# Experts' weights in a ring of 35 buffers in strict order of use, the norm's factor applied per place, two pairs put back at once

## The chip, the cores and the metric

The kernel runs on one core of one Trainium2 chip. The metric is device time in microseconds (us), the median of three runs. Engine names are those of the profile: PE (TensorE), PEld (its weight load), DVE (VectorE), ACT (ScalarE), POOL (GpSimd), SP (SyncE, whose queue issues every load and store of this kernel).

## The reference, cut to what matters

Two transformer-like blocks run one after the other on 256 tokens of width 1024, all in float32. The second ends in a mixture of experts: each token goes to the best of four groups and there to two of eight experts, so 32 experts of 1024 x 512 in all.

```
x = x + merged @ w_out
x = x + hier_moe(rms_norm_2(x, g_ffn), ...)

def hier_moe(h, w_group, b_group, w_expert, b_expert, w_gate, w_up, w_down):
    g_prob = softmax(hf @ w_group + b_group);  g_idx = argmax(g_prob)
    e_prob = softmax(the group's 8 of (hf @ w_expert + b_expert))
    top_p, top_i = top_k(e_prob, 2)
    combine = sum(one_hot(8 * g_idx + top_i, 32) * top_w)
    for e in range(32):
        hid = silu(t @ w_gate[e]) * (t @ w_up[e])
        out = out + combine[:, e:e + 1] * (hid @ w_down[e])
```

## The kernel before

The two blocks fill the first 1290 us or so of the program; there weights are loaded into five buffers `wraw`, split into a high and a low part (`whi` on ACT, `wlo` on DVE or POOL) and multiplied. The last step of the second block is the product with `w_out`, whose eight loads are the last ones ahead of the experts.

The mixture of experts is the function `moe`. Each expert has 64 places (`CAP`), and two experts make a pair `p` of 128 places, so there are 16 pairs.

- **The router** (under `HPR`) turns `x` into `Thi`/`Tlo` (`tsplit`), sums its squares (L1354), and multiplies it by the router's weights. The norm's factor `rs` is made on POOL (L291). Then a chain of some fifty DVE instructions on 2 to 64 numbers per partition finds groups, experts, weights (`comb`) and each token's rank in its expert. Its last result besides the ranks is `oi` (L1548), a flag that says whether an expert has more than 64 tokens; SP reads it into a register (`nc.values_load`, L1549), and a branch at the program's end runs the rare rest.
- **The rows to gather** are `hh` and `hl`, the high and low part of `x * g_ffn * rs`. DVE makes `x * g_ffn` into `hs` in transposed order (L1355); then `rs` is applied (`hh` on ACT, L1377; `hl` on DVE, L1378).
- **`prepare(q)`** makes one-hot matrices for two pairs, gathers their tokens by matmul into `xg`, and reads each place's weight `cg`.
- **`hidden(p)`** multiplies `xg` by the gate and up weights of two experts, 16 loads of 512 KB, and ends in a silu and a product with `cg`. **`down(p)`** transposes the result and multiplies it by the down weights, 8 loads of 512 KB. **`scatter`** puts the 128 places back into `x`.
- **`fetch`** issues such a load. Its buffer comes from `ring()`, which goes round a string of letters: 5 `wraw`, 5 `whi`, 4 `wlo`, 5 `wx`, 5 `u`, 4 `Thi`, 4 `Tlo`, in all 32 buffers, most of which the program's earlier parts use too. So 32 x 12 = 384 loads are issued by SP, in the order that the scheduler chooses by priority (`HPM`) and by when it thinks that a buffer is free.

All of SP's work is one queue: an instruction that waits holds those behind it.

Of the kernel before, what the change touches and what calls it, by code (L numbers as in the profile page):

```python
# [28 lines left out]
OP = mybir.AluOpType  # L29
# [4 lines left out]
RAW, WHI, WLO = 5, 5, 4  # L34
RAWX = 5

# [4 lines left out]
CAP = 64  # L41
RING = "w" * 5 + "h" * 5 + "l" * 4 + "x" * 5 + "u" * 5 + "T" * 4 + "t" * 4

# [76 lines left out]
def tile_model(ctx: ExitStack, tc: tile.TileContext, I: dict, out: bass.AP):  # L120
# [1202 lines left out]
    def moe(router, wb, ring):  # L1323
# [14 lines left out]

        hs, hh, hl = [unit(True), unit(True)], [runit(True), runit(True)], [runit(True), runit(True)]
        hk, hlk = ([h.rearrange("q (k p) -> q k p", k=8) for h in hx] for hx in (hh, hl))  # L1340
        hp = [h.rearrange("q (k p) -> q p k", k=8) for h in hs]
        wrs, rb = router
# [4 lines left out]
        with tc.high_priority(HPR):  # L1347

            for c in range(2):
                for t in range(2):  # L1350
                    cs = slice(512 * c, 512 * c + 512)
                    tsplit(x[:, t, cs], t, pair[c])
                    sq = wtile([128, 512], F32, name="th")
                    S.activation(sq, x[:, t, cs], AF.Square, accum_out=ss[:, t, c:c + 1])  # L1354
                    V.tensor_mul(hp[t][:, 64 * c:64 * c + 64, :], x[:, t, cs].rearrange("q (p k) -> q p k", k=8),  # L1355
                                 wb[:, cs].rearrange("q (p k) -> q p k", k=8))
            ps = psum.tile([128, 512], F32, name="proj", bufs=3)
            for K in range(8):
# [45 lines left out]
            m32 = wtile([128, 2, 32], F32R, name="m32", bufs=1)  # L1404
            comb = R_(32, "comb")

            def spread(dst, src):
                for t in range(2):
                    V.tensor_tensor(dst[:, t].rearrange("p (g e) -> p g e", g=4),
                                    ohg[:, t, :, None].to_broadcast([128, 4, 8]),  # L1410
                                    src[:, t, None, :].to_broadcast([128, 4, 8]), op=OP.mult)

            spread(m32, member)
            pc = psum.tile([128, 512], F32, name="proj", bufs=3)
# [18 lines left out]
        def prepare(q):  # L1433

            oh = wtile([128, 2, 4, CAP], F32R, name="oh", bufs=1)
            for t in range(2):
                full = [128, 4, CAP]
                V.tensor_tensor(oh[:, t], cnt_row[:, None, :].to_broadcast(full),
                                rank[:, t, 4 * q:4 * q + 4, None].to_broadcast(full), op=OP.is_equal)
            ohv = oh.rearrange("p t a s -> p t (a s)")  # L1440
            xg = []
            for k0 in range(0, 8, 2):
                if k0 % 4 == 0:
                    xg.append(unit().rearrange("p (k s) -> p k s", k=4))
                tp = psum.tile([128, 4, 128], F32, name="tp", bufs=2).rearrange("p (k a) s -> p k (a s)", k=2)
                for k in range(2):
                    for n, (src, t) in enumerate(((hk, 0), (hlk, 0), (hk, 1), (hlk, 1))):
                        mm(tp[:, k, :], src[t][:, k0 + k, :], ohv[:, t], n == 0, n == 3)
                (S.copy if k0 % 4 else V.tensor_copy)(xg[-1][:, k0 % 4:k0 % 4 + 2, :], tp)
            got = []  # L1450
            for a in range(2):
                rows = [ohv[:, t, 128 * a:128 * a + 128].bitcast(F32) for t in range(2)]
                tp = psum.tile([128, 4, 128], F32, name="tp", bufs=2)
                for t in range(2):
                    T.transpose(tp[:, t, :], rows[t], ident)
                for t in range(2):
                    mm(tp[:, 2, 0:2], rows[t], comb[:, t, 4 * q + 2 * a:4 * q + 2 * a + 2], t == 0, t == 1)
                ohT = wtile([128, 2, 128], F32R, name="ohT", bufs=4)
                S.copy(ohT, tp[:, 0:2])
                cg = wtile([128, 1], F32, name="cg", bufs=4)  # L1460
# [3 lines left out]
            return got  # L1464

        def fetch(nme, e, i):
            with tc.high_priority(HPM):
                w = ring()
                src = I[nme][0, e]
                if nme == "w_down_2":  # L1470
                    nc.sync.dma_start(w, src.rearrange("(p k) n -> p k n", k=4)[:, i])
                else:
                    nc.sync.dma_start(w.rearrange("p (j n) -> p j n", j=2),
                                      src.rearrange("(p a j) n -> p a j n", a=4, j=2)[:, i])
            return w
# [3 lines left out]
        def hidden(p, xg, a, cg):  # L1479
# [9 lines left out]
            hid = wtile([128, 512], F32, name="th")  # L1489
            S.activation(hid, pg, AF.Silu)  # L1490
            V.scalar_tensor_tensor(hid, hid, cg, pu, op0=OP.mult, op1=OP.mult)  # L1491
            return hid

        def down(p, hid):
            tp = psum.tile([128, 4, 128], F32, name="tp", bufs=2)
            hv = hid.rearrange("s (p k) -> s k p", k=4)
            for k in range(4):
                T.transpose(tp[:, k, :], hv[:, k, :], ident)
            hT = wtile([128, 4, 128], F32, name="hT", bufs=2)
            S.copy(hT, tp)  # L1500
# [11 lines left out]

        def scatter(yh, yl, ohT):
# [14 lines left out]

        ready, back = prepare(0), None
        for p in range(16):  # L1530
            xg, a, cg, ohT = ready.pop(0)
            hid = hidden(p, xg, a, cg)
            if back is not None:
                scatter(*back)
            if not ready and p < 15:
                ready = prepare(p // 2 + 1)
            back = *down(p, hid), ohT
        scatter(*back)
        store()

# [9 lines left out]
        with tc.If(flag > 0):  # L1550
            V.tensor_scalar(rank, rank, float(CAP), None, op0=OP.is_gt)
            V.tensor_mul(comb, comb, rank)
            turn, mine = wtile([128, 1], F32, name="turn", bufs=1), R_(32, "mine")
# [9 lines left out]
            with tc.For_i(0, 32) as e:  # L1563
                V.tensor_scalar(turn, turn, 1.0, None, op0=OP.add)
                V.tensor_scalar(tm, cnt_row[:, 0:32], turn[:, 0:1], None, op0=OP.is_equal)
                V.tensor_tensor(mine, comb, tm[:, None, :].to_broadcast([128, 2, 32]), op=OP.mult)
                V.tensor_reduce(cw, mine, axis=AX.X, op=OP.add)
                at = lambda nme: I[nme][0, bass.ds(e, 1)].rearrange("o a b -> (o a) b")
                for t in range(2):
# [10 lines left out]
                    hid = wtile([128, 512], F32, name="th")  # L1580
                    S.activation(hid, pg, AF.Silu)
                    V.scalar_tensor_tensor(hid, hid, cw[:, t:t + 1], pu, op0=OP.mult, op1=OP.mult)
                    hT = wtile([128, 4, 128], F32, name="hT", bufs=2)
                    tp = psum.tile([128, 4, 128], F32, name="tp", bufs=2)
# [15 lines left out]
    def run_moe(router, wb):  # L1600
# [8 lines left out]
                     t=lambda: flat(act.tile([128, 4, 256], F32, name="Tlo", bufs=4)),  # L1609
                     x=lambda: extra.tile([128, 1024], F32, name="wx", bufs=RAWX), u=unit)  # L1610
        turns = [0]
# [44 lines left out]
```

## Time and profile before

| What | Value |
|---|---|
| Time, median of 3 runs | 1817.86 us (1817.31 to 1818.43) |
| The profiled execution: own time, span | 1818.63 us, 1816.9 us |
| PE busy | 1696.3 us (93%) |
| DVE, ACT, POOL busy | 1029.8, 714.2, 324.9 us |
| Read from HBM over the span | 387.50 MB, 214 GB/s in the mean |
| SP's loads, share of 16 DMA engines | 62.8% |

The span runs from the first instruction to the last; the own time is what the run of that execution reported, 1.73 us more. PE's busy time is partly modelled: a PE that waits for weights in small steps is shown as busy.

### The profile page before, as it was taken

The numbers are of one execution on the slowest core, as the hardware profiler recorded it, in microseconds if no ns is written. First come the engines' busy times: TensorE is split into PE (matmuls) and PEld (weight loads), VectorE is DVE, ScalarE is ACT, GpSimd is POOL, SyncE is SP. The second block draws the span as 40 slices with busy tenths as digits, with TensorE's granted clock in tenths as the row PEclk, the third lists the DMA queues.
The fourth block names the chain that finished last, engine by engine and source line by source line (L and its number), as shares of the span: only waits on it lengthen the run. The fifth ranks groups of instructions, "written<-read, shape, count | busy, mean of one in ns | idle before, by whom it ended". The sixth has DMA issues, their size and how long they took to land.

```text
span 1816.9 us, 24162 instructions
## 1 busy us (share of the span) xinstructions
PE 1696.3 (93%) x9005; PEld 1262.6 (69%) x9005; DVE 1029.8 (57%) x1664; ACT 714.2 (39%) x1359; POOL 324.9 (18%) x247
## 2 busy tenths in 40 slices
PE   7999999999999999999998988867799999999997
PEld 6999888888798899888877767745644343343332
DVE  7656657656664577765768899798712121121121
ACT  5556555645444655655546452413311110110010
POOL 1111117120102002311034443464200000000000
PEclk9999999999999999999999999988899999999999
DMA  8645454465466443453745533124799999999993
GB/s 251 194 133 149 135 152 123 139 197 166 142 185 202 134 138 118 122 174 111 233 165 170 154 93 94 47 93 144 277 382 379 409 409 407 409 408 409 407 380 154
DMA packets 186105, 390.17 MB, mean 215 GB/s; under 512 B 28609, under 2 KB 66689, under 8 KB 185985
## 3 DMA queue, kind: packets, MB, share of 16 engines
q1 hardware_dynamic: 185984, 388.60, 62.8%
q8 instruction: 72, 1.18, 0.3%
q14 instruction: 49, 0.39, 0.1%
HBM read 387.50 MB, written 1.05 MB: 214 GB/s over the span
## 4 chain that ended last, share of the span: by engine, by line
PE 74%; DVE 10%; DMA 10%; issue 2%; POOL 2%; ACT 1%; SPq 0%; DVEq 0%; ACTq 0%; POOLq 0%
PE proj L146 54%; PE sc L146 10%; PE pv L146 5%; DMA u<-in_w_gate_dram 3%; DMA wraw<-in_w_gate_dram 2%; PE tp L146 2%; DVE wlo L214 2%; PE tp L362 1%; PE tp L283 1%; DMA whi<-in_w_gate_dram 1%; DVE u L934 1%; DMA wraw<-in_w_in_dram 1%; DMA wlo<-in_w_up_dram 1%; DMA wlo<-in_w_down_dram 1%; DMA Tlo<-in_w_gate_dram 1%
## 5 line engine op out<-in xcount | busy, mean ns | idle before, releaser
L213 ACT CAST whi<-wraw 128x1024 fp32r<-128x1024 f32 x336 | 352.0, 1052 | 317.6 <-PE proj L146 274.8
L214 DVE TENSOR_TENSOR wlo<-wraw,whi 128x1024 fp32r<-128x1024 f32 (+1 forms) x285 | 372.0, 1308 | 169.1 <-PE proj L146 117.2
L146 PE MATMUL proj<-wlo,Thi 128*128 128x512 f32 (+1 forms) x1056 | 418.4, 397 | 5.8 <-DVE wlo L214 5.7
L146 PE MATMUL proj<-whi,Thi 128*128 128x512 f32 (+1 forms) x1056 | 417.8, 398 | 3.6 <-ACT P L985 1.0
L146 PE MATMUL proj<-whi,Tlo 128*128 128x512 f32 (+1 forms) x1056 | 415.2, 396 | 1.5 <-DVE Tlo L968 1.5
L146 PEld LDWEIGHTS proj<-wlo,Thi 128*128 128x128 f32 x1056 | 200.5, 190 | 47.5 <-DVE wlo L214 7.4
L146 PEld LDWEIGHTS proj<-whi,Thi 128*128 128x128 f32 x1056 | 200.8, 190 | 45.5 <-DVE u L1270 2.2
L146 PEld LDWEIGHTS proj<-whi,Tlo 128*128 128x128 f32 x1056 | 200.5, 190 | 42.5 <-DVE Tlo L968 2.1
L214 POOL TENSOR_TENSOR wlo<-wraw,whi 128x1024 fp32r<-128x1024 f32 (+1 forms) x51 | 131.1, 2570 | 422.4 <-PE proj L146 346.1
L146 PE MATMUL proj<-Thi,wlo 128*128 128x256 f32 x576 | 163.9, 286 | 4.6 <-DVE wlo L214 4.6
L146 PE MATMUL proj<-Thi,whi 128*128 128x256 f32 x576 | 163.0, 287 | 4.1 <-ACT Thi L955 2.3
L146 PE MATMUL proj<-Tlo,whi 128*128 128x256 f32 x576 | 162.7, 286 | 0.0
L1510 DVE TENSOR_TENSOR u<-sc,u 128x512 fp32r<-128x512 f32 x32 | 22.1, 691 | 190.5 <-ACT u L1509 190.2
L146 PEld LDWEIGHTS proj<-Thi,wlo 128*128 128x128 f32 x576 | 111.5, 194 | 5.0 <-DVE wlo L214 4.8
L146 PEld LDWEIGHTS proj<-Thi,whi 128*128 128x128 f32 x576 | 110.5, 193 | 5.9 <-ACT Thi L955 2.9
L146 PE MATMUL sc<-u 128*128 128x256 f32 (+1 forms) x416 | 100.0, 357 | 12.8 <-DVE u L927 12.8
L146 PEld LDWEIGHTS proj<-Tlo,whi 128*128 128x128 f32 x576 | 110.6, 193 | 0.1
L1491 DVE SCALAR_TENSOR_TENSOR th<-th,cg,proj 128x512 f32<-128x512 f32 x16 | 12.0, 748 | 162.1 <-PE proj L146 102.0
L146 PEld LDWEIGHTS sc<-u 128*128 128x128 f32 x416 | 69.6, 196 | 20.7 <-issue 12.9
L1490 ACT ACTIVATE th<-proj 128x512 f32<-128x512 f32 x16 | 9.6, 597 | 185.1 <-PE proj L146 185.1
L353 ACT ACTIVATE P<-sc,nm 128x256 f32<-128x256 f32 (+1 forms) x152 | 63.7, 432 | 33.2 <-DVE nm L346 20.2
L1509 ACT CAST u<-sc 128x512 fp32r<-128x512 f32 x32 | 18.7, 586 | 101.5 <-PE sc L146 91.4
(455 smaller groups left out, 2520.6 us busy)
## 6 DMA issues: line engine op xcount, KB each, us to landing
wraw<-in_w_in_dram SPq DMA_DIRECT2D x236, 512.0 KB, 3.8
wraw<-in_w_proj_dram SPq DMA_DIRECT2D x48, 512.0 KB, 4.3
wraw<-in_w_out_dram SPq DMA_DIRECT2D x24, 512.0 KB, 4.1
wx<-in_w_up_dram SPq DMA_DIRECT2D x24, 512.0 KB, 10.2
wraw<-in_w_gate_dram SPq DMA_DIRECT2D x24, 512.0 KB, 10.2
whi<-in_w_gate_dram SPq DMA_DIRECT2D x24, 512.0 KB, 8.9
u<-in_w_up_dram SPq DMA_DIRECT2D x24, 512.0 KB, 10.2
wx<-in_w_down_dram SPq DMA_DIRECT2D x20, 512.0 KB, 10.2
```

Of the source, the lines that this page charges most:

```text
L146: T.matmul(o, l, r, start=start, stop=stop)
L213: S.copy(hi[:, :, :n], raw[:, :, :n])
L214: (G if share[0] and scount[0] % share[0] == 0 else V).tensor_sub(lo[:, :, :n], raw[:, :, :n], hi[:, :, :n].bitcast(F32))
L283: T.transpose(ps[:, b, :], src[:, b * 128:(b + 1) * 128], ident)
L353: S.activation(P[:, i * nS:(i + 1) * nS], scv[:, i, :], AF.Exp, bias=nm[:, i:i + 1], accum_out=l_out[:, i:i + 1])
L362: T.transpose(tp[:, j, :], P[:, j * 128:(j + 1) * 128], ident)
L934: V.tensor_tensor(v2(B), v2(m), st, op=OP.mult)
L1490: S.activation(hid, pg, AF.Silu)
L1491: V.scalar_tensor_tensor(hid, hid, cg, pu, op0=OP.mult, op1=OP.mult)
L1509: S.copy(yh[:, c], po[c])
L1510: V.tensor_sub(yl[:, c], po[c], yh[:, c].bitcast(F32))
```

## The change

- The ring has 35 buffers: two new ones of their own (`we`), allocated at the program's start on the other side of the memory, then 4 `wx`, 6 `u`, 5 `wraw`, 5 `whi`, 4 `wlo`, 4 `Thi`, 4 `Tlo`, and the row `rowb` that held `g_ffn`.
- Every `fetch` depends on the one before it, so that the scheduler must issue them in the program's order, which is the order of use.
- `rs` is no longer applied to the rows. `hh`/`hl` are the parts of `x * g_ffn` alone, made on POOL (two instructions a quarter) and ACT (one), and `rs` is carried to each place by a third column of `c3`: silu takes it as its scale, and the place's weight is multiplied by it. `hs` goes.
- `scatter` puts two pairs back at once (pairs 14 and 15 one by one), with one addition into `x` instead of two. `hT` has one buffer instead of two.

```diff
-RAWX = 5
+RAWX, RAWE = 4, 2
-RING = "w" * 5 + "h" * 5 + "l" * 4 + "x" * 5 + "u" * 5 + "T" * 4 + "t" * 4
+RING = "e" * 2 + "x" * 4 + "u" * 6 + "w" * 5 + "h" * 5 + "l" * 4 + "T" * 4 + "t" * 4 + "b"
...
+    early = ctx.enter_context(tc.tile_pool(name="early", bufs=1, side="right"))
...
-                    V.tensor_mul(hp[t][:, 64 * c:64 * c + 64, :], x[:, t, cs].rearrange("q (p k) -> q p k", k=8),
-                                 wb[:, cs].rearrange("q (p k) -> q p k", k=8))
...
+            for c in range(2):
+                for t in range(2):
+                    cs = slice(512 * c, 512 * c + 512)
+                    xw = wtile([128, 512], F32, name="th")
+                    xv = xw.rearrange("q (k p) -> q k p", k=8)
+                    G.tensor_tensor(xv, x[:, t, cs].rearrange("q (p k) -> q k p", k=8),
+                                    wb[:, cs].rearrange("q (p k) -> q k p", k=8), op=OP.mult)
+                    ps_ = slice(64 * c, 64 * c + 64)
+                    S.copy(hk[t][:, :, ps_], xv)
+                    G.tensor_tensor(hlk[t][:, :, ps_], xv, hk[t][:, :, ps_].bitcast(F32), op=OP.subtract)
...
-            for t in range(2):
-                S.mul(hh[t], hs[t], rs[:, t:t + 1])
-                V.scalar_tensor_tensor(hl[t], hs[t], rs[:, t:t + 1], hh[t].bitcast(F32), op0=OP.mult, op1=OP.subtract)
...
+            c3 = wtile([128, 2, 16, 3], F32, name="c3", bufs=1)
+            comb = c3[:, :, :, 0:2]
+            for t in range(2):
+                V.tensor_copy(c3[:, t, :, 2:3], rs[:, t:t + 1, None].to_broadcast([128, 16, 1]))
...
+                cg = wtile([128, 2], F32, name="cg", bufs=4)
+                V.tensor_copy(cg[:, 1:2], tp[:, 2, 2:3])
                 for j in range(2):
-                    V.tensor_copy(cg[64 * j:64 * j + 64], tp[64 * j:64 * j + 64, 2, j:j + 1])
+                    js = slice(64 * j, 64 * j + 64)
+                    V.tensor_tensor(cg[js, 0:1], tp[js, 2, j:j + 1], cg[js, 1:2], op=OP.mult)
...
+            if last:
+                tc.add_manual_dep(d.ins, last[-1].ins.name, mybir.DependencyInfo(
+                    mybir.DependencyClass.NoSync, mybir.DependencyReason.DATA), reason="order of use")
+            last.append(d)
...
-            S.activation(hid, pg, AF.Silu)
-            V.scalar_tensor_tensor(hid, hid, cg, pu, op0=OP.mult, op1=OP.mult)
+            S.activation(hid, pg, AF.Silu, scale=cg[:, 1:2])
+            V.scalar_tensor_tensor(hid, hid, cg[:, 0:1], pu, op0=OP.mult, op1=OP.mult)
...
-                    mm(ps, ohT[:, t], yh[:, c], True, False)
-                    mm(ps, ohT[:, t], yl[:, c], False, True)
+                    for n, ((yh, yl), ohT) in enumerate(ys):
+                        mm(ps, ohT[:, t], yh[:, c], n == 0, False)
+                        mm(ps, ohT[:, t], yl[:, c], False, n == len(ys) - 1)
...
-            if back is not None:
-                scatter(*back)
+            if p % 2 == 0 and back or p == 15:
+                scatter(back)
+                back = []
```

What the scheduler makes of it is seen in the order of the instructions. SP's queue from the middle of `w_out`'s loads on, before; `x5` is five such rows in a run, and 17 more loads of the experts' gate and up weights stand where the line of dots is:

```order
L1473 DMA wx<-in_w_up_dram 128x1024 x2
L1471 DMA wx<-in_w_down_dram 128x1024 x3
L198 DMA wraw<-in_w_out_dram 128x2x512 x2
L1326 DMA upper_f<-in_c_upper_dram 128x128
L1334 DMA cnt_row<-in_c_count_dram 128x64
L198 DMA wraw<-in_w_out_dram 128x2x512 x3
L1473 DMA wraw<-in_w_gate_dram 128x1024 x2
L1473 DMA wraw<-in_w_up_dram 128x1024 x2
...
L1473 DMA Thi<-in_w_up_dram 128x1024
L1549 TENSOR_LOAD oi
L1549 ISA x2
L1471 DMA u<-in_w_down_dram 128x1024 x5
```

The same place in the changed kernel; the two loads into `we` stand far ahead, among the first loads of the program:

```order
L1488 DMA we<-in_w_gate_dram 128x1024 x2
...
L1488 DMA wx<-in_w_up_dram 128x1024 x2
L1488 DMA wx<-in_w_gate_dram 128x1024 x2
L199 DMA wraw<-in_w_out_dram 128x2x512 x2
L1327 DMA upper_f<-in_c_upper_dram 128x128
L1335 DMA cnt_row<-in_c_count_dram 128x64
L199 DMA wraw<-in_w_out_dram 128x2x512 x3
L1572 TENSOR_LOAD oi
L1572 ISA x2
L1488 DMA u<-in_w_up_dram 128x1024 x2
```

The read of the flag has moved ahead of the experts' seventh load: 27 of them stood in front of it, now 6 do, and the other 378 stand behind it.

POOL's last rows before the branch, before (`wlo` belongs to `w_out`):

```order
L214 TENSOR_TENSOR wlo<-wraw,whi 128x1024
L1337 MEMSET wts 128x1 x8
L214 TENSOR_TENSOR wlo<-wraw,whi 128x1024 x4
L291 TENSOR_TENSOR rstd_11959<-rstd,neghalf 128x2
L1549 TENSOR_LOAD oi
```

And in the changed kernel, where `th` is the product and `u` the low part:

```order
L215 TENSOR_TENSOR wlo<-wraw,whi 128x1024 x4
L1368 TENSOR_TENSOR th<-x,rowb 128x512 x2
L292 TENSOR_TENSOR rstd_11970<-rstd,neghalf 128x2
L1372 TENSOR_TENSOR u<-th,u 128x8x64 x2
L1368 TENSOR_TENSOR th<-x,rowb 128x512 x2
L1372 TENSOR_TENSOR u<-th,u 128x8x64 x2
L1572 TENSOR_LOAD oi
```

Eight instructions that read two tensors each are new on POOL, two of them ahead of the norm's factor and six behind it, while the router's chain runs on DVE. ACT's rows of that stretch, before:

```order
L1354 ACTIVATE th,ss_11895<-x 128x512 x2
L284 ACTIVATE Thi<-tp 128x4x128 x2
L1377 ACTIVATE u<-u,rstd_11959 128x1024 x2
L1366 COPY lgT<-proj 72x256
L1383 ACTIVATE t_11977<-t_11977 128x8
L1394 ACTIVATE pe<-pe 128x16
L1449 COPY u<-tp 128x512 x2
```

And in the changed kernel, where the four casts are `hh`:

```order
L1354 ACTIVATE th,ss_11894<-x 128x512 x2
L285 ACTIVATE Thi<-tp 128x4x128 x2
L1371 CAST u<-th 128x8x64
L1374 COPY lgT<-proj 72x256
L1371 CAST u<-th 128x8x64
L1388 ACTIVATE t_11984<-t_11984 128x8
L1399 ACTIVATE pe<-pe 128x16
L1371 CAST u<-th 128x8x64 x2
```

The multiplication by `rs` ahead of `lgT` has gone, one cast stands there, and the last two casts, for which the last two subtractions on POOL wait, stand behind the router's second exponential.

## Rows read from the trace of the kernel before

**Rows 1.** The page: GB/s moved in 40 equal slices of the span.

```profile
GB/s 251 194 133 149 135 152 123 139 197 166 142 185 202 134 138 118 122 174 111 233 165 170 154 93 94 47 93 144 277 382 379 409 409 407 409 408 409 407 380 154
```

**Rows 2.** Busy time by stretch: PE, PEld, DVE, ACT, POOL, PEclk, DMA share, GB/s.

```profile
1450.00:1500.00 50.00, 48.35 (x226) 22.75 (x224) 11.06 (x21) 6.00 (x11) 0.00 (x0) 1.00 1.03 409
...
1785.00:1790.00 5.00, 4.91 (x21) 1.87 (x18) 2.22 (x4) 1.17 (x2) 0.00 (x0) 1.00 0.29 118
```

**Rows 3.** Chain that ended last, near the end: start, us, what.

```profile
1763.62 15.67 PE proj L146 x72
1780.70 7.09 PE sc L146 x32
```

**Rows 4.** Timeline of SP's queue, 1254 to 1320 us: start, us, instruction.

```profile
1254.82 0.81 SPq L1473 DMA_DIRECT2D wx<-in_w_up_dram  x2
1255.68 1.66 SPq L1471 DMA_DIRECT2D wx<-in_w_down_dram  x3
...
1266.95 8.96 SPq L198 DMA_DIRECT2D wraw<-in_w_out_dram  x3
1277.78 8.64 SPq L1473 DMA_DIRECT2D wraw<-in_w_gate_dram  x2
...
1308.49 0.33 SPq L1473 DMA_DIRECT2D Thi<-in_w_up_dram  x1
1316.69 3.01 SPq L1471 DMA_DIRECT2D u<-in_w_down_dram  x5
```

**Rows 5.** Waits of SP's queue, 1300 to 1320 us: total, times, longest.

```profile
SPq L1549 <- DVE oi L1548: 6.6, 1, 6.6
```

**Rows 6.** Line L1471, the load issued at 1316.69 us: time to its landing.

```profile
DMA to landing us min/median/max: 4.0/4.0/4.0
```

**Rows 7.** Timelines of the router's chain: start, us, engine, line, operation.

```profile
1302.74 0.70 POOL L291 TENSOR_TENSOR rstd<-rstd,neghalf 128x2 f32<-128x2 f32 x1 [11.00 <-DVE rstd L289]
...
1303.47 2.19 ACT L1377 ACTIVATE u<-u,rstd 128x1024 fp32r<-128x1024 f32 x2 [0.36 <-POOL rstd L291]
...
1304.66 2.48 DVE L1378 SCALAR_TENSOR_TENSOR u<-u,rstd 128x1024 fp32r<-128x1024 f32 x2 [0.71 <-ACT u L1377]
1307.05 0.41 DVE L1375 SCALAR_TENSOR_TENSOR lg<-tp,rstd,wrb 128x36 f32<-128x36 f32 x2
...
1315.48 0.15 DVE L1548 CAST oi<-om 128x1 int32<-128x1 f32 x1
```

**Rows 8.** Timelines of DVE and POOL where both read two tensors.

```profile
1289.15 2.59 POOL L214 TENSOR_TENSOR wlo<-wraw,whi 128x1024 fp32r<-128x1024 f32 x1 [0.76 <-PE proj L146]
...
1289.40 0.68 DVE L1292 TENSOR_TENSOR x<-x,proj 128x512 f32<-128x512 f32 x1
1290.60 2.09 DVE L1355 TENSOR_TENSOR u<-x,rowb 128x512 f32<-128x512 f32 x1
1299.71 1.10 DVE L1355 TENSOR_TENSOR u<-x,rowb 128x512 f32<-128x512 f32 x1
...
1162.42 1.05 POOL L914 TENSOR_TENSOR u<-cs 128x512 f32<-128x512 f32 x1 [1.23 <-DVE u L934]
...
1164.56 1.26 POOL L916 TENSOR_TENSOR u<-u 128x512 f32<-128x512 f32 x1
...
1162.26 3.64 DVE L878 TENSOR_TENSOR u<-s5t 64x64 f32<-64x64 f32 x4
...
829.60 2.39 POOL L214 TENSOR_TENSOR wlo<-wraw,whi 128x1024 fp32r<-128x1024 f32 x1 [22.89 <-PE proj L146]
...
829.75 2.26 DVE L350 TENSOR_TENSOR nm<-nm,sk 128x2 f32<-128x2 f32 x1
```

**Rows 9.** Groups by line and shape: POOL on 512 columns; count, busy us, mean ns.

```profile
L916 POOL TENSOR_TENSOR u<-u 128x512 f32<-128x512 f32 x16 | 24.3, 1517 | 1.2
```

**Rows 10.** Timelines of the end: the last down product, and the store.

```profile
1803.42 3.60 PE L146 MATMUL sc<-Tlo,hT 128*64 128x512 f32 x16
...
1809.00 2.12 SPq L1527 DMA_DIRECT2D out_dram<-x  x4
```

More of the change, by code (lines that the diff above doesn't have):

```diff
@@ L1337, in moe @@
             G.memset(wts[:, e:e + 1], float(8 - e))
-        hs, hh, hl = [unit(True), unit(True)], [runit(True), runit(True)], [runit(True), runit(True)]
+        hh, hl = [runit(True), runit(True)], [runit(True), runit(True)]
         hk, hlk = ([h.rearrange("q (k p) -> q k p", k=8) for h in hx] for hx in (hh, hl))
-        hp = [h.rearrange("q (k p) -> q p k", k=8) for h in hs]
         wrs, rb = router
@@ L1456, in prepare @@
                 for t in range(2):
-                    mm(tp[:, 2, 0:2], rows[t], comb[:, t, 4 * q + 2 * a:4 * q + 2 * a + 2], t == 0, t == 1)
+                    mm(tp[:, 2, 0:3], rows[t], c3[:, t, 2 * q + a], t == 0, t == 1)
                 ohT = wtile([128, 2, 128], F32R, name="ohT", bufs=4)
                 S.copy(ohT, tp[:, 0:2])
-                cg = wtile([128, 1], F32, name="cg", bufs=4)
+                cg = wtile([128, 2], F32, name="cg", bufs=4)
+                V.tensor_copy(cg[:, 1:2], tp[:, 2, 2:3])
                 for j in range(2):
-                    V.tensor_copy(cg[64 * j:64 * j + 64], tp[64 * j:64 * j + 64, 2, j:j + 1])
+                    js = slice(64 * j, 64 * j + 64)
+                    V.tensor_tensor(cg[js, 0:1], tp[js, 2, j:j + 1], cg[js, 1:2], op=OP.mult)
                 got.append(([(xg[k // 4], k % 4) for k in range(8)], 128 * a, cg, ohT))
             return got
+        last = []
         def fetch(nme, e, i):
@@ L1498, in down @@
                 T.transpose(tp[:, k, :], hv[:, k, :], ident)
-            hT = wtile([128, 4, 128], F32, name="hT", bufs=2)
+            hT = wtile([128, 4, 128], F32, name="hT", bufs=1)
             S.copy(hT, tp)
@@ L1511, in down, with scatter @@
             return yh, yl
-        def scatter(yh, yl, ohT):
+        def scatter(ys):
             for c in range(2):
@@ L1527, in store @@
                     nc.sync.dma_start(out[0, t * 128:(t + 1) * 128, cs], x[:, t, cs])
-        ready, back = prepare(0), None
+        ready, back = prepare(0), []
         for p in range(16):
@@ L1532, in moe @@
             hid = hidden(p, xg, a, cg)
-            if back is not None:
-                scatter(*back)
+            if p % 2 == 0 and back or p == 15:
+                scatter(back)
+                back = []
             if not ready and p < 15:
                 ready = prepare(p // 2 + 1)
-            back = *down(p, hid), ohT
-        scatter(*back)
+            back.append((down(p, hid), ohT))
+        scatter(back)
         store()
@@ L1551, in moe @@
             V.tensor_scalar(rank, rank, float(CAP), None, op0=OP.is_gt)
-            V.tensor_mul(comb, comb, rank)
+            left = R_(32, "left")
+            V.tensor_tensor(left.rearrange("p t (q c) -> p t q c", c=2), comb,
+                            rank.rearrange("p t (q c) -> p t q c", c=2), op=OP.mult)
+            for t in range(2):
+                V.tensor_tensor(left[:, t], left[:, t], c3[:, t, 0, 2:3].to_broadcast([128, 32]), op=OP.mult)
             turn, mine = wtile([128, 1], F32, name="turn", bufs=1), R_(32, "mine")
@@ L1565, in moe @@
                 V.tensor_scalar(tm, cnt_row[:, 0:32], turn[:, 0:1], None, op0=OP.is_equal)
-                V.tensor_tensor(mine, comb, tm[:, None, :].to_broadcast([128, 2, 32]), op=OP.mult)
+                V.tensor_tensor(mine, left, tm[:, None, :].to_broadcast([128, 2, 32]), op=OP.mult)
                 V.tensor_reduce(cw, mine, axis=AX.X, op=OP.add)
@@ L1580, in moe @@
                     hid = wtile([128, 512], F32, name="th")
-                    S.activation(hid, pg, AF.Silu)
+                    S.activation(hid, pg, AF.Silu, scale=c3[:, t, 0, 2:3])
                     V.scalar_tensor_tensor(hid, hid, cw[:, t:t + 1], pu, op0=OP.mult, op1=OP.mult)
-                    hT = wtile([128, 4, 128], F32, name="hT", bufs=2)
+                    hT = wtile([128, 4, 128], F32, name="hT", bufs=1)
                     tp = psum.tile([128, 4, 128], F32, name="tp", bufs=2)
@@ L1609, in run_moe @@
                      t=lambda: flat(act.tile([128, 4, 256], F32, name="Tlo", bufs=4)),
-                     x=lambda: extra.tile([128, 1024], F32, name="wx", bufs=RAWX), u=unit)
+                     x=lambda: extra.tile([128, 1024], F32, name="wx", bufs=RAWX),
+                     e=lambda: early.tile([128, 1024], F32, name="we", bufs=RAWE),
+                     b=lambda: const.tile([128, 1024], F32, name="rowb", bufs=1), u=unit)
         turns = [0]
```

16 lines of the change are left out of this document (8 added, 8 removed).

## The prediction

> **What bounds the kernel now.** I read the slices of the page first. From the 30th of 40 on the core moves 379 to 409 GB/s, and before that seldom half of it [rows 1]. That stretch is the experts' stage, and in its middle 409 GB/s are moved with the DMA share at 1.03 [rows 2]. A load has 512 KiB, so one takes 524288 / 409000 = 1.282 us, and the 24 loads of a pair take 30.8 us. PE needs less: the 64 instruction rows of `hidden` are 64/72 of a piece of the chain of 15.67 us, 13.9 us, and `down` is 7.09 us [rows 3]. With transposes and gathers that stays below 30.8 us, though the page shows PE as busy at 93%. So the stage is bound by loads: its end is the time at which the queue starts to run without a break, plus 1.282 us a load, plus what follows the last one.
>
> Then SP's queue. Before the flag 5 loads are issued at 1254.82 to 1257.3 us and 22 from 1277.78 to 1308.49 us [rows 4]. There SP stands for 6.6 us, since the read of `oi` waits for DVE [rows 5]; `oi` is done at 1315.48 + 0.15 = 1315.63 us [rows 7], and the next load goes out at 1316.69 us [rows 4], 1.06 us later, and lands 4.0 us after its issue [rows 6]. From there 357 loads without a break would end at 1316.69 + 4.0 + 356 x 1.282 = 1777.1 us. In the trace the last bytes come at about 1786.4 us (118 GB/s over 5 us are 0.59 MB, 1.4 us of a full queue) [rows 2]: some 9.3 us were lost where the queue waited for a buffer that PE was not yet done with. And 30.5 us lie between those bytes and the end of the span, since the last loads were not the last ones needed.
>
> **What the order of use gives.** Now the last eight loads are those of the last `down`. When the last one lands, half of the last piece of 16 `down` rows is left, 3.60 / 2 = 1.8 us, and from the end of that piece to the end of the span it is 1816.9 - 1807.02 = 9.9 us, in which evictions, the last scatter and the store lie [rows 10]. Nothing of that is changed for the last pair. So 11.7 us follow the last landing instead of 30.5: a gain of 18.8 us. The 9.3 us of lost queue time should go as well: a load now waits for the buffer of the load 35 places ahead, 45 us of queue, while a pair takes 30.8 us. I take all of it; at worst it stays.
>
> **What the flag takes.** In the new order 6 loads stand ahead of the flag's read and 378 behind it. The last load of `w_out` is issued by 1266.95 + 8.96 = 1275.9 us [rows 4]; from there to the flag SP issues nothing, though buffers are free. Before, 27 loads were ahead of it. So 21 loads have to be made up, 21 x 1.282 = 26.9 us. Against 18.8 + 9.3 = 28.1 us that is a gain of 1.2 us, if the flag comes when it came before. The whole change therefore hangs on the time of `oi`: each us by which it moves, moves the end.
>
> **When the flag comes.** Two things come off its chain: the multiplication by `rs` on ACT, 2.19 us, which stood ahead of `lgT`, and on DVE 2.48 us, which stood ahead of `lg` [rows 7]. `lg` could start when PE's transposes are done, about 1.0 us sooner. One thing is put in: POOL's second product is released by the same square that releases the small sum `r1s`, and the norm's factor stands behind it on POOL (it ran at 1302.74 us for 0.70 us [rows 7]); that costs about one POOL instruction less what was waited for anyway, some 1.0 us. I let these two cancel.
>
> The rest is a collision. A DVE instruction that reads two tensors in SBUF does not run beside a POOL instruction that does. A DVE product of 128x512 took 1.10 us alone and 2.09 us when it was issued inside a POOL subtraction of 2.59 us, while an addition that reads PSUM took 0.68 us inside the same subtraction; an operation on 2 numbers took 2.26 us inside another one [rows 8]. When POOL's instructions follow each other without a break, DVE gets one in at each seam: four products on 64 columns, begun just ahead of three POOL instructions of 1.05 to 1.26 us, took 3.64 us together [rows 8]. The Trainium skill says the same of it ("SBUF — State Buffer", section "Who interferes with whom"): the two share a pair of ports, and whichever starts first has it for its whole instruction. By that rule alone each POOL instruction would cost its full length.
>
> From `lg` at 1307.05 us to `oi` the router has 53 small DVE instructions, 31 of which read two tensors in SBUF. Of POOL's eight new instructions the first two lie ahead of it and the third beside `Tlo`, which reads PSUM. Five fall on it: a subtraction that waits for the cast behind `lgT`, two products, and two subtractions whose casts wait for the second exponential. Their length is not in the trace. POOL takes 1.05 us for 512 columns in the shortest row [rows 8] and 1.52 us in the mean of a group [rows 9]; these read in steps of eight columns, for which DVE took 1.10 us instead of 0.68 [rows 8], 1.6 times as long, so at most 1.7 us. I take 1.4 us, nearest to the rows with other work beside them. Of each, about 0.3 us is no loss, since a step or two of the chain get through at the seam. That is 5 x 1.1 = 5.5 us. Bounds: nothing, if the small ones slip through (and then the 1.0 us of the chain is won), and 5 x 1.7 + 1.0 = 9.5 us. By the skill's rule without a seam it would be 5 x 1.4 = 7.0 us, and the sum below would end 1.5 us later.
>
> **The sum.** Flag at 1315.63 + 5.5 = 1321.1 us; first load 1.06 us later, at 1322.2; landed at 1326.2; 377 more x 1.282 = 483.3, so the last at 1809.5; plus 1.8 and 9.9: the span is 1821.2 us. With the 1.73 us around the span the own time is 1822.9 us, against 1818.63: 4.3 us more. The runs' median is 0.77 us below that execution, so it comes to **1822 us**, 0.2% above 1817.86.
>
> What I cost at nothing: half of `scatter`'s additions gone, the scale in silu, `cg`, `c3` and `hT` with one buffer (all on DVE and ACT, which are busy for 11 and 6 of 50 us in that stage [rows 2], beside loads of 30.8 us a pair); the gathers of `prepare`, which now wait for POOL's last subtraction, at worst until 1320 us, while the loads land from 1326 on. If PE fell behind by more than 14 us (45 less 30.8), that cover would be gone and SP would wait for buffers again. Two loads more among the first of the program cost nothing where the queue has room (251 of 409 GB/s in the first slice [rows 1]) and at most 2 x 1.282 = 2.6 us.
>
> **Rivals.** *The collision is small* (36%, together with all cases from no delay to 4.8 us, which is where slower begins). For it: DVE's steps on 2 to 32 numbers are short, and several may pass at a seam. Against it: the operation on 2 numbers that took 2.26 us. With the flag 1.0 us sooner the span is 1814.7 and the median 1815.7; with 2 us of delay 1818.7. That would be no difference.
>
> *The flag holds nothing up* (5%). If the loads went on at 1277 us, the queue would run full from about 1290, when `w_out`'s last buffers come free: with 14 loads landed by then, 1293 + 369 x 1.282 + 11.7 = 1777.8 us of span, a median near 1779, 2.1% faster. Against it stand the 6.6 us in which SP waited for that very flag. A smaller gain (4%) is left if the collision is absent and the queue somewhat faster than 409 GB/s.
>
> *The queue still waits for buffers* (10%, within slower). `u` has 16 buffers that rows, outputs and loads share, and the outputs of two pairs are now held until they are put back; SP, which may no longer pass a load, would stand. If as much is lost as before, 9.3 us, the median is 1831. It decides for slower from 1 us on, if the collision costs what I take.
>
> So slower by over 0.2% has 55%, of which the collision alone 45%; within 0.2% (3.6 us, about what a measurement of this kernel can tell from no change) 36%; faster 9%. The range runs from 1815 (no delay) to 1829 (9.5 us of delay and the early loads' 2.6, or most of the 9.3 us lost); the likeliest case alone spans 1820 to 1826.
>
> **What would show it.** Right: SP idle from about 1276 us until `oi`, which is later than 1319 us; DVE operations of 0.2 us that take over 1 us, each ending with a POOL instruction; then 408 to 410 GB/s to the last load, and about 12 us from its landing to the end. Wrong: `oi` at 1316 us or sooner (no collision), loads issued between 1277 and 1315 us (the flag holds nothing), or gaps in the loads after 1330 us (buffers).

## The result, and the profile after

The changed kernel takes 1827.94 us (median of 5 runs) against 1818.43 us in runs beside it: a ratio of 1.0054, 95% interval 1.0039 to 1.0068. It is slower, as forecast, and inside the stated range (1815 to 1829), but by 9.5 us where the prediction's sum had 4.

The page's slices, after (as [rows 1]): the 29th, with 11 GB/s, is the time in which SP stands before the flag, and behind the restart 411 to 412 GB/s are kept up to the last slice.

```profile
GB/s 264 191 138 146 132 161 119 141 195 168 145 182 199 133 140 115 127 184 101 234 169 165 145 103 82 53 86 144 11 377 411 411 412 411 411 412 412 412 411 293
```

SP's queue around the flag (timeline, as [rows 4]; then its longest wait, as [rows 5]: total, times, longest):

```profile
1268.13 8.96 SPq L199 DMA_DIRECT2D wraw<-in_w_out_dram  x3
1324.67 1.31 SPq L1488 DMA_DIRECT2D u<-in_w_up_dram  x2
...
SPq L1572 <- DVE oi L1571: 46.3, 1, 46.3
```

Before, that wait was 6.6 us. POOL and DVE while it lasts (timelines, as [rows 7]), POOL first:

```profile
1301.75 4.00 POOL L1368 TENSOR_TENSOR th<-x,rowb 128x512 f32<-128x512 f32 x2 [8.85 <-ACT th L1354]
...
1306.53 1.28 POOL L1372 TENSOR_TENSOR u<-th,u 128x512 fp32r<-128x512 f32 x1
1309.02 1.26 POOL L1372 TENSOR_TENSOR u<-th,u 128x512 fp32r<-128x512 f32 x1 [1.22 <-ACT u L1371]
1310.24 3.92 POOL L1368 TENSOR_TENSOR th<-x,rowb 128x512 f32<-128x512 f32 x2
1316.41 2.48 POOL L1372 TENSOR_TENSOR u<-th,u 128x512 fp32r<-128x512 f32 x2 [2.24 <-ACT u L1371]
```

```profile
1301.65 0.69 DVE L1293 TENSOR_TENSOR x<-x,proj 128x512 f32<-128x512 f32 x1 [0.80 <-PE proj L147]
1303.19 0.62 DVE L1376 TENSOR_TENSOR r1s<-ss 128x2 f32<-128x2 f32 x1 [0.85 <-ACT th L1354]
1303.84 1.93 DVE L290 TENSOR_SCALAR rstd<-r1s 128x2 f32<-128x2 f32 x1
...
1306.89 0.96 DVE L1414 COPY c<-rstd 128x16 f32<-128x16 f32 x1
1309.39 0.42 DVE L1383 SCALAR_TENSOR_TENSOR lg<-tp,rstd,wrb 128x36 f32<-128x36 f32 x2 [1.54 <-PE tp L147]
...
1310.41 1.83 DVE L1299 TENSOR_TENSOR ohg<-lg,r 128x8 f32<-128x8 f32 x1
1312.17 0.15 DVE L1387 TENSOR_TENSOR t<-lg,r 128x8 f32<-128x8 f32 x1
1312.28 1.91 DVE L1300 TENSOR_TENSOR ohg<-ohg,wts 128x8 f32<-128x8 f32 x1
...
1316.47 0.17 DVE L1298 TENSOR_REDUCE r<-pe 128x2 f32<-128x16 f32 x1
1316.67 1.03 DVE L1299 TENSOR_TENSOR oh<-pe,r 128x16 f32<-128x16 f32 x1
1317.73 1.19 DVE L1300 TENSOR_TENSOR oh<-oh,wts 128x16 f32<-128x16 f32 x1
...
1323.46 0.15 DVE L1571 CAST oi<-om 128x1 int32<-128x1 f32 x1
```

Read the two side by side. POOL's two products take 1.96 us each, from 1310.24 us. DVE's comparison of 1310.41 us, on 8 numbers, takes 1.83 us and ends at 1312.24, with the first product; one step of 0.15 us slips through at the seam, and the next is held to 1314.19, the end of the second product. The same follows with the two subtractions of 1.24 us at 1316.41. Between the two, from 1314.2 to 1316.6 us, no step takes over 0.35 us.

Steps that read only one tensor are held too: the norm's `rstd` (2 numbers, 1.93 us) ends at 1305.77 us, 0.02 us after the second of the first two products, and a copy of `rs` (16 numbers, 0.96 us) ends at 1307.85 us, 0.04 us after the first subtraction. With no POOL instruction beside them (e1) the first takes 0.17 us, and this copy and the next together 0.24. A reduction of 0.17 us ran inside the subtraction of 1316.41 us and was not held.

PE's first product on an expert's weights, before and after, and the last two `down` pieces after (timelines):

```profile
1320.58 3.98 PE L146 MATMUL proj<-wraw,u 128*64 128x512 f32 x16
...
1328.57 2.23 PE L147 MATMUL proj<-we,u 128*64 128x512 f32 x8
...
1806.84 5.37 PE L147 MATMUL sc<-Thi,hT 128*64 128x512 f32 x16 [0.73 <-ACT hT L1520]
1812.02 3.65 PE L147 MATMUL sc<-Tlo,hT 128*64 128x512 f32 x16
```

From PE's first product to the end of the last `down` piece I call **PE's stretch**. After, it is 1815.67 - 1328.57 = 487.1 us, and 10.5 us follow; before, it went from 1320.58 to 1807.02 us, 486.4 us [rows 10 for its end], and 9.9 followed. So of the 9.3 us between the spans (1826.2 and 1816.9) 8.0 lie ahead of PE's first product, and next to nothing in the sixteen pairs: waits of one kind have gone there and others have come.

The first two loads behind the flag, issued at 1324.67 and 1325.06 us, and the last load, issued at 1802.54 us (time to landing, as [rows 6]; SP's timeline):

```profile
DMA to landing us min/median/max: 4.0/6.0/8.0
...
1798.70 4.17 SPq L1486 DMA_DIRECT2D Tlo<-in_w_down_dram  x4
DMA to landing us min/median/max: 10.0/10.0/10.0
```

So the first lands at 1328.7 us and the last at 1812.6 us.

### The profile page after: what moved, and what is told of

It reads as the page before. It is cut to its first block, busy times and chain, and to the rows that moved or that the text cites. A ratio compares the mean times of both kernels' runs of the same rounds, so it can differ in the third digit from the quotient of the medians.

```text
span 1826.2 us, 24103 instructions
## 1 busy us (share of the span) xinstructions
PE 1695.3 (93%) x9005; PEld 1259.1 (69%) x9005; DVE 1017.2 (56%) x1648; ACT 714.0 (39%) x1361; POOL 335.9 (18%) x253
## 4 chain that ended last, share of the span: by engine, by line
PE 72%; DVE 11%; DMA 11%; issue 2%; POOL 2%; ACT 1%; SPq 1%; DVEq 0%; ACTq 0%; POOLq 0%
PE proj L147 52%; PE sc L147 9%; PE pv L147 5%; PE tp L147 2%; DVE wlo L215 2%; PE tp L363 1%; PE tp L284 1%; DMA whi<-in_w_up_dram 1%; DMA wraw<-in_w_up_dram 1%; DMA wlo<-in_w_up_dram 1%; DMA u<-in_w_down_dram 1%; DMA wraw<-in_w_in_dram 1%; DMA Tlo<-in_w_down_dram 1%; DMA Tlo<-in_w_up_dram 1%; DMA Thi<-in_w_up_dram 1%
## 5 line engine op out<-in xcount | busy, mean ns | idle before, releaser
L1510 ACT ACTIVATE th<-proj,cg 128x512 f32<-128x512 f32 x16 | 11.0, 687 | 195.4 <-PE proj L147 195.3
```

Source lines behind the costliest of these rows:

```text
L1510: S.activation(hid, pg, AF.Silu, scale=cg[:, 1:2])
```

## The experiments

Each ratio is to runs of the kernel before taken beside it (their medians lie between 1817.39 and 1818.43 us). "PE's stretch" is read as above from the one profiled execution, to which "oi done" and "span" belong too; all times in us.

| Run | oi done | PE's stretch | its length | span | median | ratio (95%) |
|---|---|---|---|---|---|---|
| before | 1315.6 | 1320.6 to 1807.0 | 486.4 | 1816.9 | 1818.43 | |
| changed | 1323.6 | 1328.6 to 1815.7 | 487.1 | 1826.2 | 1827.94 | 1.0054 (1.0039 to 1.0068) |
| e1 POOL late | 1315.6 | 1332.6 to 1809.6 | 476.9 | 1819.3 | 1822.73 | 1.0025 (1.0014 to 1.0035) |
| e2 flag last | - | 1330.8 to 1807.8 | 477.0 | 1817.4 | 1818.67 | 1.0003 (0.9992 to 1.0013) |
| e3 both | - | 1333.4 to 1809.9 | 476.4 | 1819.6 | 1820.66 | 1.0019 (1.0010 to 1.0028) |
| e4 free order | 1325.5 | 1330.5 to 1827.0 | 496.5 | 1836.3 | 1838.47 | 1.0112 (1.0097 to 1.0128) |
| e5 before + order | 1315.5 | 1320.5 to 1811.5 | 491.0 | 1821.7 | 1824.23 | 1.0037 (1.0023 to 1.0051) |
| e6 the same, flag last | - | 1321.9 to 1812.4 | 490.5 | 1822.7 | 1824.51 | 1.0039 (1.0025 to 1.0053) |
| e7 flag last, cover | - | 1329.4 to 1799.0 | 469.6 | 1808.5 | 1811.38 | 0.9967 (0.9955 to 0.9979) |
| e8 e7 + rows early | - | 1322.1 to 1788.0 | 465.9 | 1798.0 | 1798.62 | 0.9893 (0.9878 to 0.9908) |
| e9 e2, one pair back | - | 1332.2 to 1835.2 | 503.0 | 1845.1 | 1845.21 | 1.0143 (1.0130 to 1.0156) |
| e10 no early loads | 1323.8 | 1328.7 to 1815.4 | 486.7 | 1825.5 | 1827.66 | 1.0054 (1.0039 to 1.0069) |
| e11 e8, flag back | 1316.9 | 1321.6 to 1808.4 | 486.7 | 1818.3 | 1820.35 | 1.0015 (1.0005 to 1.0025) |
| e12 changed + cover | 1325.8 | 1330.8 to 1818.3 | 487.6 | 1828.2 | 1829.14 | 1.0054 (1.0040 to 1.0068) |

**e1: POOL's eight instructions behind the flag.** The block of `th` products is moved behind `oi`, and its products wait for it.

```diff
+                    tc.add_manual_dep(gp.ins, rk.ins.name, mybir.DependencyInfo(
+                        mybir.DependencyClass.Sync, mybir.DependencyReason.DATA), reason="behind the router")
```

> The changed kernel with POOL's eight products and subtractions made to wait for the flag, so that none of them runs beside the router's chain on DVE; the strict order and the flag's place, behind six loads, stay. Theory (the flag holds 378 loads back, and POOL delays the flag): the 5.6 us by which the chain from lg to oi grew and the 1.3 us ahead of lg go, oi is done near 1316.7 us, the loads restart 6.9 us sooner and the whole ends 6.9 us sooner, at a median of about 1821 us. The rows are ready some 5 us later than in the changed kernel, which the 35 buffers hide. Rival (the delay is not POOL's, or PE's start sets the end): oi near 1323 us, or the time at 1827 us or more.

POOL's and DVE's timelines in this run, and SP's wait for PE from 1325 to 1815 us (total, times, longest):

```profile
1315.75 3.92 POOL L1444 TENSOR_TENSOR th<-x,rowb 128x512 f32<-128x512 f32 x2 [11.53 <-DVE oi L1429]
...
1307.68 0.17 DVE L1299 TENSOR_TENSOR ohg<-lg,r 128x8 f32<-128x8 f32 x1
...
1315.45 0.15 DVE L1429 CAST oi<-om 128x1 int32<-128x1 f32 x1
...
SPq L1496 <- PE proj L147: 14.4, 15, 5.6
```

The comparison that took 1.83 us takes 0.17; from `lg` (1307.03 us) to `oi` it is 8.6 us again, as before the change, instead of 14.2. So the collision is the delay of the flag. The flag comes 8.0 us sooner, not 6.9; the last load lands 5.0 us sooner (1807.6 us), the profiled span is 6.9 us shorter and the median 5.2. The span's 6.9 is the number expected, but by luck: here the loads alone no longer set the end. PE begins 4.1 us later than in the changed kernel, since its rows are ready later, and from there it needs 476.9 us, as in e2 below; it waits for no load ahead of the last `down` piece (4.91 us there instead of 3.65), while SP waits for PE 14.4 us in all. That the flag's delay is passed on to the end in full is not shown. A POOL product alone takes 1.96 us as well: that length is its own.

**e2: the flag read behind the last load.**

```diff
-        V.tensor_copy(oi, om)
+        oc = V.tensor_copy(oi, om)
+        tc.add_manual_dep(oc.ins, last[-1].ins.name, mybir.DependencyInfo(
+            mybir.DependencyClass.NoSync, mybir.DependencyReason.DATA), reason="flag behind the loads")
```

> The changed kernel with the flag's cast, and so its read, put behind the last expert load; all else as it is, the collision on POOL too. Theory (the flag's place in SP's queue is what costs): the loads go on at 1278 us, all 35 buffers are full by about 1322 us, the first comes free when PE begins pair 0 at about 1329 us, and 349 loads from there at 1.28 us and 13.6 us behind the last one give a span of 1793 us and a median near 1795 us, 1.3% below before. Rival (the loads wait for something else, for buffers or because of the strict order): no gain, 1820 to 1828 us.

Neither: 1818.67 us, 9 us better than the changed kernel and 24 worse than my number. The loads did go on at 1278 us, and the 35 buffers were full at 1326.6 us (the 35th load, issued at 1316.47 us, landed 10.1 us later). SP's timeline and PE's waits (total, times, longest) in PE's stretch, 1340 to 1800 us:

```profile
1316.47 0.33 SPq L1488 DMA_DIRECT2D rowb<-in_w_up_dram  x1
1332.74 0.33 SPq L1488 DMA_DIRECT2D we<-in_w_up_dram  x1
...
PE tp L1518 <- DVE th L1511: 15.1, 16, 1.2
PE pv L147 <- ACT u L1529: 9.9, 15, 0.7
PE sc L147 <- ACT hT L1520: 2.6, 8, 0.7
```

The next load waits until 1332.74 us, for PE to be done with the first buffer. PE waits for no load here, and still needs 477.0 us, 29.8 a pair. It waits for silu and its product at each of the 16 transposes, for the cast of the outputs at nearly each pair, and for the copy `hT`. This is a second floor that I had not priced: in the order that the change makes, PE's pairs take 29.8 us, only about 1 us less than a pair's loads.

**e3: both edits.** The edits of e1 and e2; POOL's block waits for the last step ahead of `oi`, since `oi` itself is now late.

> The two edits together: the flag read behind the last load, and POOL's eight instructions behind the router's chain. Theory: with the flag out of the queue the collision no longer counts by the flag but only by when PE can begin pair 0; the rows are ready at about 1327 us on POOL and the first product starts near 1333 us, 4 us later than with the flag last alone, so the median is about 4 us above that one, near 1799 us. Rival (DVE's delay by itself is what costs): 5 to 7 us below the one with the flag last alone.

1820.66 us, 2 us above e2: PE's first product is 2.7 us later and its stretch as long. As the theory said, with the flag out of the queue only PE's start counts; its level, 1799 us, was missed as in e2.

**e4: the changed kernel without the dependency between loads.**

```diff
-            if last:
-                tc.add_manual_dep(d.ins, last[-1].ins.name, mybir.DependencyInfo(
-                    mybir.DependencyClass.NoSync, mybir.DependencyReason.DATA), reason="order of use")
```

> The changed kernel without the dependency of each load on the one before it; ring, factor and scatter as they are. In SP's queue 29 loads then stand ahead of the flag's read instead of 6. Theory: oi stays late, at about 1323.5 us, but 355 loads are behind it instead of 378, so the last landing would be 23 x 1.28 = 29 us sooner with no new waits; the free order gives back part of it in waits for buffers and in the tail (in the kernel before 9 and 19 us). So 1798 us at best, up to 1825 us if all of it is given back. Rival (the strict order itself is what gains, the flag's place is nothing): slower than the changed kernel, above 1830 us.

1838.47 us, outside what the theory allowed and on the rival's side. The loads were done at 1803.6 us, 9 us sooner than in the changed kernel, but 32.7 us lay behind the last one, and PE waited 32 us for loads (6.8 us the longest) that stood behind others needed later. So in this kernel the order is worth 10 us, though it puts 23 loads more behind the flag.

**e5: the kernel before with the order alone**, the dependency of the change's diff in its `fetch`; **e6: the same with the flag last**, as in e2.

> The kernel before, with one thing of the change alone: each expert load depends on the one before it. Ring, factor, scatter and POOL as before; in SP's queue 19 loads now stand ahead of the flag's read instead of 27. Theory after the first four runs (PE in the order hidden, transposes, down of the same pair needs 476.9 us from its first expert product to its last, 29.8 a pair, about 3 of them pauses): PE starts as before at 1320.6 us, ends at 1797.5, and with 10 us behind that the span is 1807.5 us, the median about 1808.5, 0.5% below before. Rival (the prediction's: loads alone set the end): 364 loads behind the flag, the first landed at 1320.7, 3 us lost at the restart, 1790.5 + 11.7, a span of 1802 us and a median near 1803 us. If the order itself costs nothing and brings nothing: 1818 us.

> The one before, and the flag read behind the last load as well. Theory (PE's 476.9 us from its first product): the queue no longer matters, PE starts at 1320.6 us or 1 us later, so the same time as with the order alone, a median of 1808 to 1810 us. Rival (loads alone set the end): all 32 buffers full by about 1322 us, 352 loads from 1325.7 us on, a span near 1789 us and a median near 1790 us, 1.5% below before.

The numbers for e5 (1808.5, 1803, 1818 us) were all wrong: alone, the order makes the kernel before slower by 6.8 us. e6's number (1808 to 1810) was wrong with it, but that e6 takes the same time as e5, as its theory said, shows that the queue no longer matters there. PE's waits in its stretch, in e5:

```profile
PE tp L1504 <- DVE th L1497: 13.0, 14, 0.9
PE sc L146 <- ACT hT L1506: 10.1, 14, 0.7
PE pv L146 <- ACT u L1515: 8.6, 13, 0.7
```

Before, PE waited 0.9 us once for `th`, 8.5 for `hT`, and 14.5 for loads; now 31.7 for DVE and ACT, and for no load. With the loads in free order the scheduler had put another pair's products in these places. Still, 491.0 is 14 more than the 477 of e2.

**e7: cover.** On top of e2, the first four loads of the next pair and their products go ahead of this pair's eight `down` loads: the gate half ahead of the transposes, the up half behind them.

```diff
             S.copy(hT, tp)
+            if then:
+                head(then, 1)
...
-            back.append((down(p, hid), ohT))
...
+            if p < 15:
+                nxt = start(p + 1)
+                lead = head(nxt, 0)
+            back.append((down(p, hid, nxt, lead), ohT))
```

> The changed kernel with the flag read behind the last load, and with the first four loads of the next pair, and their products, moved ahead of the pair's down loads: the gate half covers the wait for silu, the up half the wait for the copy of the transposed rows. Theory (in the flag-last kernel PE set the end, through its pauses): the stage is PE's no longer but the loads': PE starts at 1330.8 us, the first reused buffer is filled at about 1336.5, 349 loads at 1.28 us, 13.6 behind them: a span of 1797 us, a median near 1798 us, 20 us below the flag-last kernel. Rival (PE's pauses are not what held it, its work is): 1818 us as there.

1811.38 us. The waits for `th` fall from 15.1 to 0.9 us, those for `hT` to 0.7, and the stretch from 477.0 to 469.6 us. The direction is the theory's, the size about a third of it (7.3 us of 20): the stage does not become the loads', since PE's work without these pauses is still 29.1 us a pair (465.9 us over 16 in e8, where PE waits for no load; here it waits 0.8 us for loads).

**e8: rows early.** As e7; two of the four quarters of `hh`/`hl` on POOL in buffers of their own (`xw`) as soon as `x` has them, two on DVE; one early buffer less.

```diff
-RAWX, RAWE = 4, 2
+RAWX, RAWE = 4, 1
...
+            for c in range(1):
...
+                    xw = wtile([128, 512], F32, name="xw")
...
+            for c in range(1, 2):
...
+                    V.tensor_tensor(xv, x[:, t, cs].rearrange("q (p k) -> q k p", k=8),
```

> As the run with the cover, and the rows to gather made without the collision: two quarters on POOL as soon as x has them, in buffers of their own (one early buffer less, ring of 34), two on DVE ahead of lg. Theory: PE's first expert product moves from 1330.8 to about 1322.5 us, the loads end as much sooner less one buffer: a span near 1789 us, a median near 1790 us, 1.5% below before. Rival (the start of PE no longer counts, the loads run from the time at which the queue opens): the same time as the run with the cover.

1798.62 us, 1.1% below before: the best of all. PE begins at 1322.1 us, 7.3 sooner than in e7, and its stretch is 3.7 shorter. The 9 us to my number go with PE's floor again: PE waits for no load, and SP waits for PE (28.6 us).

**e9: one pair put back at a time**, on e2.

```diff
-            if p % 2 == 0 and back or p == 15:
+            if back:
```

> The flag-last kernel with one pair put back at a time instead of two, all else equal. Theory (the difference between the order alone, 491 us from PE's first expert product to its last, and the flag-last kernel, 477 us, lies in putting back two pairs at once): PE's stretch grows to about 490 us and the median from 1818.7 to about 1832 us. Rival (it lies in the ring, or in the buffers of the transposed rows): 477 us and 1818 to 1820 us.

503.0 us against 477.0: putting two back at once is worth 26 us under the strict order, twice what I expected. Busy time by stretch (as [rows 2]) where one pair's transposes have nothing beside them:

```profile
1578.00:1579.00 1.00, 0.06 (x1) 0.07 (x1) 0.75 (x1) 0.00 (x0) 0.00 (x0) 1.00 0.79 274
1579.00:1580.00 1.00, 0.68 (x4) 0.49 (x4) 0.00 (x0) 0.23 (x1) 0.00 (x0) 1.00 0.89 279
1580.00:1581.00 1.00, 0.59 (x4) 0.30 (x6) 0.00 (x0) 0.36 (x1) 0.00 (x0) 1.00 1.02 360
1581.00:1582.00 1.00, 1.00 (x6) 0.26 (x4) 0.00 (x0) 0.00 (x0) 0.00 (x0) 0.67 1.02 414
1582.00:1583.00 1.00, 1.00 (x4) 0.23 (x1) 0.00 (x0) 0.00 (x0) 0.00 (x0) 0.50 1.02 414
1583.00:1584.00 1.00, 1.00 (x6) 0.43 (x5) 0.00 (x0) 0.00 (x0) 0.00 (x0) 0.50 1.02 406
1584.00:1585.00 1.00, 1.00 (x6) 0.34 (x4) 0.00 (x0) 0.00 (x0) 0.00 (x0) 0.63 1.02 418
1585.00:1586.00 1.00, 1.00 (x6) 0.33 (x4) 0.00 (x0) 0.00 (x0) 0.00 (x0) 1.00 1.04 426
```

PE pauses for `th` and again for `hT` (0.95 and 0.73 us in its timeline), then the granted clock falls to 0.50, the lower of its two levels (1.2 GHz), until about 1584.7 us. That happens in six places between 1350 and 1720 us, though all sixteen pairs have both pauses; summed over stretches of 1 us the clock lost 10.3 us in PE's stretch, in e2 nothing. What decides whether it falls is open: in e2 two pairs have the same two pauses, and it stays at 1.00. The waits for `hT` grew by 8.3 us (11.6 against 3.3, over the whole stretch). With two pairs at once some products, of the output or of the next gathers, stand between the transposes and the first `down` product. These two make 18.6 of the 26 us; the rest I did not resolve. e5 has the same two (5.2 us of clock, 6.8 of `hT`), 12 of its 14.

**e10: no early loads.**

```diff
+            if not last:
+                tc.add_manual_dep(d.ins, uf.ins.name, mybir.DependencyInfo(
+                    mybir.DependencyClass.NoSync, mybir.DependencyReason.DATA), reason="not early")
```

(`uf` is the load of `upper_f`, behind five of `w_out`'s.)

> The changed kernel with its first expert loads issued behind the sixth part of the last projection's loads, instead of among the program's first. Theory (the two early loads put off the first projection's loads by 2 us, and 1.0 us of it is still there at x's last addition): that addition comes back from 1301.65 to about 1300.7 us, oi to 1322.6 us, and the time falls by 1 us, to about 1827 us, unless the six loads now hold up the projection's last ones. Rival (the shift has another origin): x's last addition stays at 1301.6 us or later.

No difference: `x` is done 0.6 us sooner, `oi` is not. The theory is not borne out. In the changed kernel and in e12, whose programs are the same up to there, `x`'s last addition began at 1301.65 and at 1303.8 us, 2.2 us apart, so 1.0 us at that place is no evidence for anything.

**e11: e8 with the flag's read where the scheduler puts it**, e2's edit undone.

> The best kernel so far (cover, rows without the collision, ring of 34) with the flag's read back where the scheduler puts it, ahead of 379 loads. Theory (once PE no longer pauses, the queue behind the flag sets the end): oi at about 1317.5 us, first landing at 1322.6, 378 more at 1.283 us, 12 us behind the last: a span of 1819 us, a median near 1821 us, 22 us above the kernel with the flag last. Rival (the flag's place costs little, as PE sets the end): 1799 to 1803 us.

**e12: the changed kernel with e7's cover alone.**

> The changed kernel with the cover alone: the first four loads of the next pair and their products ahead of the pair's down loads; flag and POOL as in the change. Theory (in the changed kernel itself the loads set the end, PE's pauses lie beside them): no change, 1826 to 1829 us, PE's stretch 487 us with the waits for DVE and ACT turned into waits for loads. Rival (PE's pauses set the end there too): 1810 to 1818 us.

Both as the theory had them (e12 by 0.1 us outside its range). In e11 `oi` is done at 1316.9 us and the kernel takes 1820.35 us, 22 us more than with the flag last. In e12 the cover removes PE's waits for `th` as in e7, and nothing is gained: 487.6 us, 30.5 a pair, paced by the loads, which come at 411 to 412 GB/s.

## Why the prediction was right, and where its sizes were off

**The mechanism held.** Seen: SP idle from 1277 us to `oi`, DVE steps on 8 and 16 numbers of 1.0 to 1.9 us that end with a POOL instruction, 411 to 412 GB/s from the restart to the last load. The trace agrees with the rule cited from the Trainium skill ("SBUF — State Buffer", section "Who interferes with whom"): a held step ends with its POOL instruction, at 1312.24 and 1314.19 us. Between two of POOL's instructions a step of 0.15 us came through. What DVE lost behind `lg`, 5.6 us (14.2 against 8.6), is the 5.5 of the sum; e1 shows that it is POOL's doing. That agreement is partly luck, for it hides two errors: POOL's products take 1.96 us, not 1.4 and above my bound of 1.7, so that the five instructions take 7.7 us (two of 1.96, three of 1.24 to 1.26) where I had 7.0, and 2.0 us of that were no loss where I had 1.5. The loss was not even either: 0.4 us by the first subtraction, 3.4 by the two products, 1.9 by the last two subtractions.

**The terms that were off** make 5.0 us of span (1826.2 against 1821.2):
- The flag came at 1323.6 us, not 1321.1. I let the steps ahead of `lg` cancel. From the start of `x`'s last addition to `lg` it took 6.4 us before, 7.7 after, and 5.5 in e1, without POOL beside it: the 1.0 us to be won was there (0.9), but the collision ahead of `lg`, which I put at about 1.0, took 2.2. The first two products held DVE's two small steps of the norm (0.62 and 1.93 us), and `Tlo` behind them; the prediction named only steps that read two tensors, and the longer of these reads one. So `lg` came 1.3 us later. The other 1.0 us is the shift of that addition itself, which lies within what executions differ by (e10).
- From first to last landing 483.9 us, not 483.3: the loads came closer than 1.282 us (1.275 in the mean), but 3.1 us were lost at the restart (4.3 us from the first landing to the second). The trace before has the same gap, 4.0 us: of the 9.3 us that the prediction put down to buffers and took back whole, some 2.7 were this restart, and they came again.
- Behind the last landing 13.6 us, not 11.7: PE had 3.1 us of `down` left, not 1.8, and 10.5 behind it, not 9.9. The piece ahead of the last took 5.37 us, with the granted clock at 0.50 from about 1807.1 to 1810.5 us; in e2, at 1.00, it took 3.70.

**A price that was wrong.** The step "PE needs less ... so the stage is bound by loads" was true for the changed kernel (e12), but by about 1 us a pair only: 29.8 us of PE (e2) against 30.6 of loads (24 at 1.275). So the rival "the flag holds nothing up" could not give 1779 us; e2 gives 1818.67, and "wait for buffers" took another form, as SP stood because PE was not done. Nor are the 28.1 us of "what the order of use gives" a gain of the order by itself: e5, with the order alone, is slower than before, since PE's pauses take the place of its waits for loads. In the changed kernel the pauses lie beside the loads, and the sum by loads worked because the flag had made the loads late enough to be the bound.

**What was costed at nothing.** The early loads cost nothing that could be seen (e10). Putting back two pairs at once, on the list of things hidden by DVE's and ACT's idle time, was worth 26 us under the strict order without the flag (e9); in the changed kernel itself it was not tried alone, nor was `hT` with one buffer.

## What to carry to other kernels

When a queue is put in strict order, look for the one instruction in it that waits for a computation: everything behind it now waits too, and a flag that nobody needs until the end can be read behind the last load. A stage with two engines near the bound has two floors; price both before promising what freeing one will bring, and count the small pauses of the one that is ahead, since a strict order of loads also fixes the order of the work. Work put on POOL beside a chain of small DVE steps can cost the chain most of POOL's time: here 5.6 of 7.7 us behind `lg`, and 2.2 us more ahead of it.

## What the runs showed of the hardware that was not expected

- A POOL product of 512 columns read in steps of eight took 1.96 us, alone or beside DVE; the subtraction of as many columns read straight took 1.24 us.
- DVE steps that read one tensor were held to the end of a POOL instruction as well: a `TENSOR_SCALAR` on 2 numbers took 1.93 us (0.17 in e1), a copy of 16 numbers 0.96 us (two of them 0.24 in e1). A reduction of 0.17 us was not held.
- Two short pauses of PE, of about 0.95 and 0.73 us with four transposes between, were followed by 3.4 us at the lower clock in six of the sixteen such pairs of e9, and in neither of the two such pairs of e2.
- After an idle queue the second load landed 4.3 us behind the first, the next ones every 1.3 to 1.7 us (in the changed kernel). It was 4.0 us in the kernel before and 4.7 in e12, but 1.3 in e1, where the restart cost 0.7 us in all, at the third load; why is open.
